# TensorE in the order of the text in the mixing stage of a two-layer decoder trunk, with more buffers for cached keys and values

## The chip, the cores and the metric

One core of one Trainium2 chip runs the whole kernel. The metric is the time of one execution on the device in microseconds (us); lower is better. The engines are TensorE (PE, matmuls; PEld is its loading of weights), VectorE (DVE), ScalarE (ACT), GpSimd (POOL) and SyncE (SP), whose queue issues most DMAs.

## What is computed

Two layers of a decoder, for 512 prompt tokens and 64 sample tokens (8 sequences of 8 new tokens, each with 2048 cached positions), model width 1024, hidden width 2816, all in fp32. Cut to what matters:

```python
def layer(x, l, k_past, v_past, s0):
    h = x + 0.5 * rmsnorm(swiglu(rmsnorm(x, ...), w_gate, w_up, w_down), ...)
    m, k_new, v_new, s_new = token_mixing(rmsnorm(h, ...), w_in[l], ..., w_out[l], k_past, v_past, s0)
    h = h + rmsnorm(m, ...)
    h = h + 0.5 * rmsnorm(swiglu(rmsnorm(h, ...), ...), ...)
    return h, k_new, v_new, s_new

def token_mixing(hn, w_in_l, ...):
    z = hn @ w_in_l                                  # 1024 -> 3584
    aq, ak, av, bq, bf, bi, bg = split(z)            # attention q k v, HGRN2 q f i g
    outs = [dilated_window(aq, ak, av, w, d) for (w, d) in ((128, 1), (512, 4), (2048, 16))]
    o_a = rmsnorm(dilated_mixture(outs), attn_g_l)   # 8 heads of 64
    f = lb_l + (1.0 - lb_l) * sigmoid(bf)
    o_b, s_fin = hgrn2_scan(silu(bq), 1.0 - f, bi, log(f), s_init, chunk)   # 4 heads of 128
    o_b = rmsnorm(o_b, hgrn_g_l) * silu(bg)
    return concatenate([o_a, o_b]) @ w_out_l, k_new, v_new, s_fin
```

For the sample tokens the attention's keys and values are the cached ones and the new ones, and HGRN2 starts from a given state.

## The kernel before

Activations lie with the features on the partitions and the tokens in the columns, in two halves of 288 tokens (256 of the prompt and 32 of the samples). Every weight and every operand of a product is split into two float32r parts, the high part on ACT (L114) and the low part on DVE (L116). A product then takes three matmuls per 128 rows of the contraction: high by high (L353), high by low (L354) and low by high (L355); with 1024 rows that makes 24 matmuls of 128x288. Weights come as items of 128 columns, in the order of use; SP loads an item (L95) and two loads stand ahead. `WBUF` items of split weights can be held, and `XBUF` more in a pool that exists outside the mixing stage only.

A layer is SwiGLU, mixing, the output projection and SwiGLU. The mixing stage runs 28 items of w_in (`run_phase` with lag 0): each item first for one half of the tokens, then for the other, so there are 56 calls of `issue`. One `issue` writes a product, the parked transposes (`flush_late`), the next weights' loads and splits (`w_ahead`), the product's evacuation (`evac`), and then `side`. Items 0 to 11 are attention's q, k and v, 12 to 23 the f, q and i of the four HGRN2 heads, 24 to 27 their gates.

`side` is where the other work of the stage comes in, from Python generators that are pulled a few steps at a time: four steps of the sample attention (`sample`), two of each of up to two HGRN2 heads (`hgrn`), two of the prompt attention (`prompt_unit`), one of the norm of attention's output. What is left when the items run out is pulled by `rest`.

- `sample` works on two sample sequences at a time: scores `sc` (L849) against cached keys, each cached tile `kv` 128x512 (256 KB) loaded by L815 (keys) and L818 (values) into one of `KVB` buffers; scores `scn` against the new keys, also L849; a maximum (L874) and an exponential over all 1344 columns (L875); transposes `ptps` (L884); `pov`, the product with the values (L904); its scaled copy `ob` (L910) and the transpose `otr` (L913).
- `hgrn` goes through one head in levels `lev` (blocks of 1 to 8 at L590, with L594 for the samples, 32 at L623, 64 at L631). After each level DVE rescales zq (L659) and POOL rescales zk (L661), and the next level reads both. Then `ktp` (L676), its copy `kt` (L677), `kv` (L687), and the head's end with the `pos` matmuls of 8 columns (L697).
- `prompt_unit` has scores `psc` (L765), softmax, transposes `ptp` (L780), the copy `pt` (L782 on DVE, L784 on ACT) and `ppv` (L789).

The order in which each engine issues is set by the tile framework's scheduler, which places every instruction by its own estimate; the text's order only serves it as a start. In the mixing stage it puts scores, levels and transposes between the matmuls of a product.

Of the kernel before, what the change touches and what calls it, by code (L numbers as in the profile page):

```python
# [9 lines left out]

F32 = mybir.dt.float32
F32R = mybir.dt.float32r
U8 = mybir.dt.uint8
AF = mybir.ActivationFunctionType
ALU = mybir.AluOpType
# [12 lines left out]
EPS = 1e-6  # L28
LAG = 3
GRP = 4  # L30
WBUF = 4
XBUF = 4
ZBUF = 2
ABUF = 2
KVB = 5
G_OFF = {}
_o = 0
for _n, _w in (("ff1_pre_g", 8), ("ff1_post_g", 8), ("mix_pre_g", 8), ("attn_norm_g", 4), ("hgrn_norm_g", 1),
# [9 lines left out]
def trunk_step(ctx: ExitStack, tc: tile.TileContext, a, L):  # L48
# [13 lines left out]
    ps_mm = ctx.enter_context(tc.tile_pool(name="ps_mm", bufs=2, space=PSUM))  # L62
    ps_hg = ctx.enter_context(tc.tile_pool(name="ps_hg", bufs=2, space=PSUM))

# [1 line left out]
    items = []  # L66
    for l in range(L):
        ff = {}
# [56 lines left out]
        while st["dma"] < min(st["split"] + 2, len(items)):  # L125
            w_dma()

# [1 line left out]
    def const(name, shape):  # L129
        return cp.tile(shape, F32, name=name)  # L130

# [34 lines left out]
    def late_consts():  # L166
        lstage = tmp("lstage")[:, :NLM * 32].rearrange("p (a b) -> p a b", b=32)
        for n, t in (("logits", logit), ("lmask", lstage), ("pbias", pbias), ("sb_str", sb_str), ("sb_rec", sb_rec),
                     ("sb_new", sb_new), ("bmask", bmask), ("eye32", eye32)):
            sp.dma_start(t if n == "lmask" else t[:], a[n])  # L170
        dve.tensor_copy(lmask[:], lstage)
        # lower bounds of the forget gates
        dve.tensor_copy(lbm[:], logit[:, 0, :])
        for l in range(1, L):
            dve.tensor_tensor(lbm[:], lbm[:], logit[:, l, :], op=ALU.max)
        for l in range(L):
            dve.tensor_tensor(lbe[:, l, :], logit[:, l, :], lbm[:], op=ALU.subtract)
        act.activation(lbe[:], lbe[:], AF.Exp)
        dve.tensor_copy(lbs[:], lbe[:, 0, :])
        for l in range(1, L):  # L180
            dve.tensor_tensor(lbs[:], lbs[:], lbe[:, l, :], op=ALU.add)
        dve.reciprocal(lbs[:], lbs[:])
        for l in range(L):
            dve.tensor_tensor(lbe[:, l, :], lbe[:, l, :], lbs[:], op=ALU.mult)
        dve.tensor_copy(lbm[:], lbe[:, 0, :])
        for l in range(L):
            if l:
                dve.tensor_tensor(lbm[:], lbm[:], lbe[:, l, :], op=ALU.add)
            dve.tensor_tensor(fof[:, l, :], lbm[:], lbe[:, 0, :], op=ALU.subtract)
            dve.tensor_scalar(fsc[:, l, :], fof[:, l, :], -0.5, 0.5, op0=ALU.mult, op1=ALU.add)  # L190
            dve.tensor_scalar(nfs[:, l, :], fsc[:, l, :], -1.0, None, op0=ALU.mult)
            dve.tensor_tensor(fof[:, l, :], fof[:, l, :], fsc[:, l, :], op=ALU.add)
# [2 lines left out]
    def tmp(name="tmp"):  # L195
        return tp.tile([P, H], F32, name=name, tag="tmp", bufs=6)

# [1 line left out]
    def stats(acc, inv, out_psum=False, tag="rb"):  # L199
        """rsqrt of the mean square of every token, on all partitions: [128, 288]"""  # L200
        s = ps_hg.tile([P, 512], F32, name="stat", tag="hg")
        for c in range(3):
            pe.matmul(s[:96, c:c + 1], acc[:, 96 * c:96 * c + 96], ones[:, 0:1], start=True, stop=True)
        sm = tp.tile([96, 4], F32, name="sm", tag="sm", bufs=2)
        dve.tensor_scalar(sm[:, :3], s[:96, :3], inv, EPS, op0=ALU.mult, op1=ALU.add)
        pool.tensor_tensor(sm[:, :3], sm[:, :3], nhalf[:96, :3], op=ALU.pow)  # L206
        yield
        b = ps_hg.tile([P, 512], F32, name="bc", tag="hg")
        for c in range(3):
            pe.transpose(b[:, 96 * c:96 * c + 96], sm[:, c:c + 1].to_broadcast([96, P]), ident[:96, :96])  # L210
        if out_psum:
            return b[:, :H]
        rb = tp.tile([P, H], F32, name="rb", tag=tag, bufs=1)
        act.activation(rb[:], b[:, :H], AF.Copy)
        return rb[:]

    class Chain:
        """what one half of the tokens goes through between two phases, issued in steps: jn tiles of the
        next operand are there, then its scale r"""

        def __init__(self, hf, gen):
            self.hf, self.jn, self.r, self.done = hf, 0, None, False
# [116 lines left out]
            c()  # L339

    def product(group, order=None, chain=None):
        """group: (psum, item, high, low); one tile of the contraction after the other, for all of them"""
        for _, i, _, _ in group:
            w_get(i)
        k = items[group[0][1]][1]
        order = order or range(k)
        for n, j in enumerate(order):
            s = slice(j * P, (j + 1) * P)
            if chain is not None:
                chain.until(n + 1)  # L350
            for ps, i, xhi, xlo in group:
                wh, wl = whi[i], wlo[i]
                pe.matmul(ps, wh[:, s], xhi[:, j, :], start=(n == 0), stop=False)  # L353
                pe.matmul(ps, wh[:, s], xlo[:, j, :], start=False, stop=False)  # L354
                pe.matmul(ps, wl[:, s], xhi[:, j, :], start=False, stop=(n == k - 1))  # L355
            if len(group) > 1 or n == k // 2 - 1:
                hook()

    def run_phase(n, operand, evac, chains, order=None, lag=LAG, side=None, on_done=None):
        """n items from items[st.next]; operand(i, hf) gives (psum, high, low), evac(i, hf, psum) takes the product"""  # L360
        i0 = st["next"]
        st["next"] += n

        def issue(idx, hf):
            group, tiles = [], []
            if idx[0] == 0:
                chains[hf].until(1)
            for i in idx:
                pst, xhi, xlo = operand(i, hf)
                group.append((pst[:, :H], i0 + i, xhi, xlo))  # L370
                tiles.append(pst)
            first = idx[0] == 0
            product(group, order if first else None, chains[hf] if first else None)
            flush_late()
            if hf == 0:
                w_ahead(i0 + idx[-1])
            else:
                w_ahead(i0 + idx[0])
            hook()
            if first:  # L380
                chains[hf].until_r()
            for i, pst in zip(idx, tiles):
                evac(i, hf, pst)
                if i == n - 1 and on_done is not None:
                    active.append(on_done(hf))
                if side is not None:
                    side(i, hf)

        g = list(range(GRP))
        issue(g, 0)  # L390
        issue(g, 1)
        for i in range(GRP, n):
            issue([i], 0)
            if i - lag >= GRP:
                issue([i - lag], 1)
        for i in range(max(GRP, n - lag), n):
            issue([i], 1)
        flush_late()

# [1 line left out]
    def swiglu(l, w, chains, gp, mk_chain, side=None):  # L401
        with ExitStack() as es:
            hpool = es.enter_context(tc.tile_pool(name="hid", bufs=1))
# [60 lines left out]
            run_phase(n, operand, evac, chains, side=side, on_done=on_done)  # L464
        return nxt

# [1 line left out]
    def mixing(l, chains, xpool_close, x_spill):  # L468
        o = [None, None]
        with ExitStack() as es:  # L470
# [39 lines left out]
            def evac(i, hf, pst):  # L510
                ps = pst[:, :H]
                r = rn[hf]
                if i < 8:
                    dst = (aq if i < 4 else ak)[:, i % 4, hf, :]
                    dve.tensor_tensor(dst, ps, r, op=ALU.mult)
                    if i == 7 and hf == 1:
                        late.append(lambda: sp.dma_start(a["o_k"][l], ak[:]))
                    return
                t = tmp("z")
                if i < 12 or (i < 24 and i % 3 == 2):  # L520
                    dve.tensor_tensor(t[:], ps, r, op=ALU.mult)
# [27 lines left out]
                    gates.append((h, hf, t))  # L549

            gates = []
            left = [12, 12]
            gated = [0, 0]
            normed = [False, False]
# [9 lines left out]
            hg_done = set()  # L564
            stage = [0] * 4

# [1 line left out]
            def pcol(t, c):  # L568
                return t[:, c // 2, (c % 2) * P:(c % 2) * P + P]

# [163 lines left out]
                hg_done.add(h)  # L734
                stage[h] = 4

# [1 line left out]
            def prompt_unit(p, i, alt):  # L738
                n = (i + 1) * P
                if alt == 1:  # L740
# [58 lines left out]
                    yield from prompt_unit(p, i, alt)  # L799
                    left[i // 2] -= 1  # L800

# [1 line left out]
            kvq = []  # L803
            kvs = {"n": 0}

# [132 lines left out]
            def side(i, hf):  # L938
# [10 lines left out]
                if i < 8:  # L949
                    return  # L950
                if i == 11 and hf == 1:
                    flush_late()
                    flags["av"] = True
                    prm.append(prompt(0))
# [17 lines left out]
                        if not pull(g):  # L972
                            hg.remove(g)

# [1 line left out]
            oa_g = g_of(l, "attn_norm_g")  # L976

            def anorm(hf):
# [43 lines left out]
            oc = [o_chain(0), o_chain(1)]  # L1022
            run_phase(28, operand, evac, chains, lag=0, side=side, on_done=lambda hf: oc[hf])
            tail["on"] = True
            while hg or prm or smp or alt or alt2 or an or gates:
                rest()
        return oc

    def w_out(l, chains, gp, mk_chain):
# [24 lines left out]
            run_phase(NJ, operand, evac, chains, on_done=on_done)  # L1054
        return nxt

# [1 line left out]
    xs = ExitStack()  # L1058

    def x_tiles():  # L1060
# [44 lines left out]
    xs.close()  # L1105


# [1 line left out]
def _tiles(w):  # L1109
    """(..., K, M) -> (..., M/128, 128, K): one contiguous [128, K/128 * 128] block for every 128 columns"""  # L1110
    *b, K, M = w.shape
    n = len(b)
    t = w.reshape(*b, K // P, P, M // P, P)
# [2 lines left out]


def _cols(v):
    """(L, n*128) -> (128, L, n)"""
    L = v.shape[0]  # L1120
    return np.transpose(v.reshape(L, -1, P), (2, 0, 1))

# [93 lines left out]
```

## Time and profile before

| | us |
|---|---|
| three runs | 2625.37, 2623.82, 2618.42 |
| median of the runs | 2623.82 |
| span of the profiled execution | 2620.2 |
| PE busy in it | 2570.6 (98%) |
| DVE, ACT, POOL busy | 1186.3, 900.4, 384.0 |
| the two mixing stages, as read below | 326.5 and 351.9 |

The profiled execution has no time of its own beside its span; the span stands 3.6 us under the median of the runs. "Busy" is the time in which an engine has an instruction under way; matmuls overlap, so a PE that is busy all the time can still start its matmuls at a greater or a smaller spacing. The row of an instruction gives its start, its duration, the engine and line, what it writes and reads, and in brackets how long its engine stood idle before it and what ended that.

### The profile page before, as it was taken

What the parts mean: (1) busy time and instruction counts of PE and PEld (TensorE: products, weight loads), DVE (VectorE), ACT (ScalarE), POOL (GpSimd) and SP (SyncE); (2) the same over time, 40 slices, a digit from 0 to 9 for tenths busy, and PEclk for the clock granted to TensorE, in tenths of its full rate; (3) what the DMA queues carried; (4) which work ended last, traced back from release to release, by engine and by line L of the source; (5) the groups of instructions that cost most, each with busy time, mean ns of one, the idle gap of its engine ahead of it and who ended that gap; (6) DMA issues with size and microseconds to landing.
All of it is one profiled execution on the core that took longest, in us unless ns stands there. A gap on an engine that the chain in (4) does not pass through costs nothing.

```text
span 2620.2 us, 52041 instructions
## 1 busy us (share of the span) xinstructions
PE 2570.6 (98%) x21844; PEld 2401.9 (92%) x21844; DVE 1186.3 (45%) x2648; ACT 900.4 (34%) x2023; POOL 384.0 (15%) x450
## 2 busy tenths in 40 slices
PE   8999999999999999999999999999999999999997
PEld 8999999867878999999999999997677799999997
DVE  6333346235555642434563334362456556324333
ACT  5232235133335532223532322342333254323232
POOL 1101012002212210101210010110022122101012
PEclk9999999999999999999999999999999899999998
DMA  5222223475543222222222222236754442222221
GB/s 177 81 81 81 89 74 109 159 240 172 167 155 130 82 89 81 83 87 76 78 89 81 81 81 89 74 108 190 223 186 156 131 145 73 87 83 74 89 81 44
DMA packets 108604, 292.03 MB, mean 111 GB/s; under 512 B 12753, under 2 KB 16081, under 8 KB 107601
## 3 DMA queue, kind: packets, MB, share of 16 engines
q1 hardware_dynamic: 107936, 288.28, 34.0%
q8 instruction: 172, 2.82, 0.4%
q14 instruction: 64, 0.52, 0.1%
q10 hardware_dynamic: 432, 0.41, 0.1%
HBM read 272.13 MB, written 16.52 MB: 110 GB/s over the span
## 4 chain that ended last, share of the span: by engine, by line
PE 90%; DVE 4%; issue 3%; DMA 1%; POOL 1%; ACT 1%; SPq 0%; POOLq 0%; ACTq 0%; DVEq 0%
PE gu L353 13%; PE gu L354 13%; PE gu L355 13%; PE mm L353 12%; PE mm L355 12%; PE mm L354 12%; PE sc L849 2%; PE pov L904 1%; PE psc L765 1%; PE ppv L789 1%; DMA kv<-in_kc 1%; DVE y L313 1%; POOL sm L206 1%; PE ptp L780 1%; DVE x L316 1%
## 5 line engine op out<-in xcount | busy, mean ns | idle before, releaser
L353 PE MATMUL gu<-xh,whi 128*128 128x288 f32 x2752 | 813.3, 296 | 7.1 <-ACT xh L269 6.3
L354 PE MATMUL gu<-xl,whi 128*128 128x288 f32 x2752 | 813.1, 295 | 0.0
L355 PE MATMUL gu<-xh,wlo 128*128 128x288 f32 x2752 | 811.2, 295 | 0.0
L114 ACT ACTIVATE whi<-wraw 128x512 fp32r<-128x512 f32 (+1 forms) x688 | 394.9, 614 | 758.3 <-PE gu L354 360.6
L116 DVE TENSOR_TENSOR wlo<-wraw,whi 128x512 fp32r<-128x512 f32 (+1 forms) x688 | 445.3, 680 | 194.7 <-ACT whi L114 176.9
L353 PEld LDWEIGHTS gu<-xh,whi 128*128 128x128 f32 x2752 | 517.9, 188 | 8.3 <-ACT xh L269 6.7
L355 PEld LDWEIGHTS gu<-xh,wlo 128*128 128x128 f32 x2752 | 518.9, 189 | 0.0
L354 PEld LDWEIGHTS gu<-xl,whi 128*128 128x128 f32 x2752 | 517.7, 188 | 0.5 <-DVE xl L270 0.5
L353 PE MATMUL mm<-hh,whi 128*128 128x288 f32 x1408 | 415.7, 295 | 0.0
L355 PE MATMUL mm<-hh,wlo 128*128 128x288 f32 x1408 | 414.7, 295 | 0.0
L354 PE MATMUL mm<-hl,whi 128*128 128x288 f32 x1408 | 414.7, 295 | 0.0
L434 POOL TENSOR_TENSOR gate<-gate,rb 128x288 f32<-128x288 f32 x176 | 163.8, 931 | 1287.8 <-ACT gate L433 1287.8
L353 PE MATMUL mm<-xh,whi 128*128 128x288 f32 x1088 | 334.9, 308 | 1.5 <-DVE y L449 1.5
L354 PE MATMUL mm<-xl,whi 128*128 128x288 f32 x1088 | 327.3, 301 | 0.0
L355 PE MATMUL mm<-xh,wlo 128*128 128x288 f32 x1088 | 327.3, 301 | 0.0
L355 PEld LDWEIGHTS mm<-hh,wlo 128*128 128x128 f32 x1408 | 264.7, 188 | 0.0
L354 PEld LDWEIGHTS mm<-hl,whi 128*128 128x128 f32 x1408 | 264.4, 188 | 0.0
L353 PEld LDWEIGHTS mm<-hh,whi 128*128 128x128 f32 x1408 | 264.2, 188 | 0.0
L438 DVE TENSOR_TENSOR hid<-gu,gate 128x288 f32<-128x288 f32 x172 | 78.7, 457 | 332.2 <-PE gu L355 323.6
L353 PEld LDWEIGHTS mm<-xh,whi 128*128 128x128 f32 x1088 | 205.3, 189 | 25.1 <-issue 21.4
L354 PEld LDWEIGHTS mm<-xl,whi 128*128 128x128 f32 x1088 | 205.4, 189 | 12.9 <-issue 12.4
L355 PEld LDWEIGHTS mm<-xh,wlo 128*128 128x128 f32 x1088 | 205.6, 189 | 12.6 <-issue 12.1
(193 smaller groups left out, 2430.0 us busy)
## 6 DMA issues: line engine op xcount, KB each, us to landing
wraw<-in_wgu SPq DMA_DIRECT2D x175, 512.0 KB, 3.4
kv<-in_kc SPq DMA_DIRECT2D x160, 256.0 KB, 3.4
kv<-in_vc SPq DMA_DIRECT2D x160, 256.0 KB, 3.3
wraw<-in_wd SPq DMA_DIRECT2D x64, 448.0 KB, 3.3
wraw<-in_w_in SPq DMA_DIRECT2D x56, 512.0 KB, 4.2
wraw<-in_wd SPq DMA_DIRECT2D x32, 512.0 KB, 3.5
wraw<-in_w_out SPq DMA_DIRECT2D x16, 512.0 KB, 4.4
xs<-x SPq DMA_DIRECT2D x4, 1152.0 KB, 4.2
```

The source lines that it names most:

```text
L114: act.activation(whi[i][:, c], r[:, c], AF.Copy)
L116: dve.tensor_tensor(wlo[i][:, c], r[:, c], f(whi[i][:, c]), op=ALU.subtract)
L206: pool.tensor_tensor(sm[:, :3], sm[:, :3], nhalf[:96, :3], op=ALU.pow)
L313: ins = dve.tensor_tensor(y[:, js, :], y[:, js, :], rb[:, None, :].to_broadcast([P, 2, H]), op=ALU.mult)
L316: dve.tensor_tensor(x[:, js, :], x[:, js, :], y[:, js, :], op=ALU.add)
L353: pe.matmul(ps, wh[:, s], xhi[:, j, :], start=(n == 0), stop=False)
L354: pe.matmul(ps, wh[:, s], xlo[:, j, :], start=False, stop=False)
L355: pe.matmul(ps, wl[:, s], xhi[:, j, :], start=False, stop=(n == k - 1))
L434: pool.tensor_tensor(g[:], g[:], rn[hf], op=ALU.mult)
L438: dve.tensor_tensor(h[:], ps, gate[hf][:], op=ALU.mult)
L765: pe.matmul(dst, q, kk, start=True, stop=True, tile_position=(64 * s, 0))
L849: pe.matmul(ps[32 * p:32 * p + 32, c], qbd[:, 2 * bp + bb, p, :], rhs(p), start=(bb == 0), stop=(bb == 1), tile_position=(0, 32 * p))
```

## The change

PE leaves the scheduler in most of the mixing stage: from `side` of item 11, second half, until everything of the stage has been pulled, `tc.manual_schedule` makes it issue in the order of the text. All other engines stay with the scheduler. `KVB` goes from five to nine buffers, so that eight loads stand ahead at the start of `sample`. `WBUF` goes from four to three and `XBUF` from four to five. From item 24 on, `evac` pulls `rest` as long as three gates or more are waiting. The constant `END` is 1, so its branch does nothing. Line numbers rise by one up to `evac` and by four behind its new loop (L353 is L354, L849 is L853, L904 is L908).

```diff
+END = 1
...
-WBUF = 4
-XBUF = 4
+WBUF = 3
+XBUF = 5
...
-KVB = 5
+KVB = 9
...
                     return
+                while i >= 24 and len(gates) >= 3:
+                    rest()
                 t = tmp("z")
...
             gates = []
+            man = ExitStack()
...
                 if i == 11 and hf == 1:
+                    man.enter_context(tc.manual_schedule(engines={mybir.EngineType.PE}))
                     flush_late()
...
             tail["on"] = True
+            if END == 0:
+                man.close()
             while hg or prm or smp or alt or alt2 or an or gates:
                 rest()
+            man.close()
         return oc
```

What this does to PE's order, at two places of layer 0. The first is in a run of score blocks of `sample`. A row is the line, the operation, what it writes and reads, the size and how many follow each other; `mm` are the product's matmuls, `sc` the scores, two matmuls for each cached tile. Before:

```order
L849 MATMUL sc<-kv,qbd 32x256 x2
L353 MATMUL mm<-xh_4516,whi 128x288
L354 MATMUL mm<-xl_4517,whi 128x288
L849 MATMUL sc<-kv,qbd 32x256 x2
L355 MATMUL mm<-xh_4516,wlo 128x288
L353 MATMUL mm<-xh_4516,whi 128x288
L354 MATMUL mm<-xl_4517,whi 128x288
L355 MATMUL mm<-xh_4516,wlo 128x288
L353 MATMUL mm<-xh_4516,whi 128x288
L354 MATMUL mm<-xl_4517,whi 128x288
L355 MATMUL mm<-xh_4516,wlo 128x288
L849 MATMUL sc<-kv,qbd 32x256 x2
```

And with the change:

```order
L354 MATMUL mm<-xh_4516,whi 128x288
L355 MATMUL mm<-xl_4517,whi 128x288
L356 MATMUL mm<-xh_4516,wlo 128x288
L853 MATMUL sc<-kv,qbd 32x256 x16
L784 MATMUL ptp<-ident,S 128x128 x2
L793 MATMUL ppv<-pt,vt 64x128 x2
L354 MATMUL mm<-xh_4716,whi 128x288
L355 MATMUL mm<-xl_4717,whi 128x288
```

The scores of eight cached tiles now stand in one row behind a whole product, and the prompt unit's `ptp` and the `ppv` that reads its copy stand next to each other, ahead of the next product.

The second place is at the last levels of HGRN2's first head. `lev` 32x32 is the level of 32, `lev` 64x64 the level of 64 of the same head. Before:

```order
L355 MATMUL mm<-xh_4716,wlo 128x288
L904 MATMUL pov<-kv,pts 32x128 x16
L623 MATMUL lev<-zq,zk 32x32 x8
L765 MATMUL psc<-ak,aq 128x256 x2
L353 MATMUL mm<-xh_4516,whi 128x288
L354 MATMUL mm<-xl_4517,whi 128x288
L355 MATMUL mm<-xh_4516,wlo 128x288
L353 MATMUL mm<-xh_4516,whi 128x288
L354 MATMUL mm<-xl_4517,whi 128x288
L631 MATMUL lev<-zq,zk 64x64 x4
L355 MATMUL mm<-xh_4516,wlo 128x288
```

And with the change:

```order
L356 MATMUL mm<-xh_4716,wlo 128x288
L908 MATMUL pov<-kv,pts 32x128 x16
L627 MATMUL lev<-zq,zk 32x32 x8
L635 MATMUL lev<-zq,zk 64x64 x4
L769 MATMUL psc<-ak,aq 128x256 x2
L354 MATMUL mm<-xh_4516,whi 128x288
L355 MATMUL mm<-xl_4517,whi 128x288
L356 MATMUL mm<-xh_4516,wlo 128x288
```

The second level, which stood behind two scores and five matmuls of the next product, now stands directly behind the first, and the product behind both.

## Rows read from the trace of the kernel before

**Rows 1.** The page: span, and busy time of the engines.

```profile
span 2620.2 us, 52041 instructions
...
PE 2570.6 (98%) x21844; PEld 2401.9 (92%) x21844; DVE 1186.3 (45%) x2648; ACT 900.4 (34%) x2023; POOL 384.0 (15%) x450
```

**Rows 2.** Mixing stages: stretch, us, busy PE, PEld, DVE, ACT, POOL, clock, DMA, GB/s.

```profile
497.00:823.50 326.50, 319.70 (x3664) 240.19 (x3664) 160.97 (x507) 108.52 (x305) 58.66 (x85) 0.99 0.55 177
1797.00:2148.90 351.90, 344.50 (x3834) 263.16 (x3833) 173.26 (x526) 122.38 (x331) 59.12 (x83) 0.98 0.55 175
```

**Rows 3.** Timeline of PE, scores inside a product: start, duration, engine, line, operation.

```profile
501.53 0.29 PE L353 MATMUL mm<-xh,whi 128*128 128x288 f32 x1
501.75 0.63 PE L849 MATMUL sc<-kv,qbd 128*32 128x256 f32 x4
502.31 0.40 PE L354 MATMUL mm<-xl,whi 128*128 128x288 f32 x1
502.54 0.30 PE L355 MATMUL mm<-xh,wlo 128*128 128x288 f32 x1
502.68 0.29 PE L353 MATMUL mm<-xh,whi 128*128 128x288 f32 x1
```

**Rows 4.** Timeline of PE, sixteen score passes in one piece.

```profile
650.76 1.07 PE L849 MATMUL sc<-kv,qbd 128*32 128x256 f32 x16
651.76 0.38 PE L210 MATMUL bc<-ident,sm 96*128 96x96 f32 x2
```

**Rows 5.** Timeline of PE, ppv inside a product.

```profile
609.20 0.65 PE L789 MATMUL ppv<-pt,vt 128*64 128x128 f32 x6
609.78 0.40 PE L355 MATMUL mm<-xh,wlo 128*128 128x288 f32 x1
610.02 0.29 PE L353 MATMUL mm<-xh,whi 128*128 128x288 f32 x1
```

**Rows 6.** Timeline of PE and DVE, from one level to the next of one head.

```profile
613.80 0.43 PE L623 MATMUL lev<-zq,zk 128*32 128x32 f32 x16
...
615.33 0.58 DVE L626 COPY A<-lev 32x128 f32<-32x128 f32 x2
...
615.92 0.49 DVE L659 TENSOR_TENSOR zq<-zq,d 128x128 f32<-128x128 f32 x2
...
616.36 0.42 PE L631 MATMUL lev<-zq,zk 128*64 128x64 f32 x4 [0.64 <-DVE zq L659]
```

**Rows 7.** Timeline of PE and DVE, a prompt unit's transpose and its copy.

```profile
607.86 0.33 PE L780 MATMUL ptp<-ident,S 128*128 128x128 f32 x1
...
608.23 0.42 DVE L782 COPY pt<-ptp 128x256 f32<-128x256 f32 x1
```

**Rows 8.** Timeline of PE and ACT, from scn over the exponential to ptps.

```profile
584.57 0.39 PE L849 MATMUL scn<-ak,qbd 128*32 128x64 f32 x10
...
585.82 1.42 ACT L875 ACTIVATE ss<-ss,smx 128x1344 f32<-128x1344 f32 x1 [0.51 <-DVE smx L874]
...
588.45 0.38 PE L884 MATMUL ptps<-ident,ss 128*128 128x128 f32 x2
```

**Rows 9.** Timeline of PE, a score that waited for its cached tile.

```profile
642.37 0.62 PE L849 MATMUL sc<-kv,qbd 128*32 128x256 f32 x4 [0.70 <-DMA kv<-in_kc]
```

**Rows 10.** The page, DMA issues: count, KB each, median us to landing.

```profile
kv<-in_kc SPq DMA_DIRECT2D x160, 256.0 KB, 3.4
```

**Rows 11.** PE in a short stretch: us, busy (count), granted clock, DMA share, GB/s.

```profile
2044.00:2057.00 13.00, 13.00 (x44) 0.50 0.41 133
```

**Rows 12.** Timeline of PE, ahead of that stretch and in it.

```profile
2040.82 1.95 PE L697 MATMUL pos<-zq,s 128*128 128x8 f32 x16
...
2053.22 0.44 PE L355 MATMUL mm<-xh,wlo 128*128 128x288 f32 x1
2053.46 0.44 PE L353 MATMUL mm<-xh,whi 128*128 128x288 f32 x1
```

## The prediction

> **What bounds the kernel now.** I read the head of the page first: the profiled execution spans 2620.2 us and TensorE (PE) is busy for 98% of it [rows 1]. Then the table of stretches, for the two mixing stages, the only places that the change touches: they last 326.5 and 351.9 us, and PE is idle for only 6.8 and 7.4 us of them [rows 2]. So the scheduler's order hides nearly every wait of the attention and HGRN2 chains behind product matmuls. Its price must be looked for inside the busy time, and the timeline shows it. Two product matmuls follow each other at .14 us (502.54 to 502.68). Where four score passes are put between them, 501.53 to 502.54 holds two products' spacing and the visit: 1.01 - .28 = .73 us [rows 3]. Sixteen score passes in one piece cost 1.00 us from their start to the next matmul, and .22 - .14 = .08 to get in, 1.08 us or .27 per four [rows 4]. (The trace shows a score matmul as two passes, so four passes are two matmuls, which read one cached tile.) A split visit thus costs .46 us more than its share of a gathered one, .23 per edge. After the other kinds an edge is cheaper: a product that follows ppv holds the next one off by .24 in place of .14, .10 more [rows 5].
>
> **What the change takes away.** Counted in the two lists of orders, per layer: the products stand in 110 pieces before and 56 after; runs of scores fall from 54 to 29; changes from one kind of matmul to another from 425 to 288, 137 fewer. Of these edges, 50 to 52 are of scores at .23 us, 12 us; the other 85 to 89 at .10, 9 us. Gain 21 us; all at .08 it is 11, all at .23 it is 32. Of PE's own 7 us of waiting I count 5 as gone (0 to 7), since the score block's loads now have eight tiles of lead. **Gain per layer 26 us, bounds 11 and 39.**
>
> **What it adds: waits that nothing covers.** In text order PE stops at each matmul whose operand is not there, and what stands behind it, the next product first of all, waits too, although it is ready. VectorE (DVE) and ScalarE (ACT) are 45% and 34% busy, so they don't bind; it is the latency of one chain that counts. I counted the pairs in which a matmul now stands right behind the one that feeds it, and took the price from the same chain in the trace of before.
> - *Level behind level of the same HGRN2 head*, 16 per layer: side pulls each head twice, so two levels stand next to each other, and the second reads the zq and zk that the first one's successors rescale. At 613.80 the level's passes run until 614.23, the copy and the rescaling on DVE take .58 and .49, and the next level starts at 616.36 [rows 6]. Bounds: the two DVE instructions alone, 1.07 us, and the whole gap, 2.13. I take 1.3, near the low end, because in that row other work stood ahead on DVE and will less often when PE itself waits: 21 us (17 to 34).
> - *ptp, then ppv* of a prompt unit, 16 per layer against 3: the copy of the transposed tile takes .42 on DVE; from the end of ptp at 608.19 to ppv at 609.20 it is 1.01 [rows 5, 7]. I take .7: 11 us (7 to 16).
> - *scn, then ptps* of a pair of sample batches, 3 per layer against none: a reduction and an exponential over 1344 columns lie between. The exponential alone takes 1.42 us, the whole gap is 588.45 - 584.96 = 3.49 [rows 8]. I take 2.5: 8 us (4 to 10).
> - *pov, ob, otr*, 8 per layer against none, and *ktp, kt, kv*, 4 per layer: a copy each, which I price by the .42 of the one between ptp and ppv [rows 7]; the wider kt has the two short ktps matmuls beside it. 12 x .42: 5 us.
> - *Cached keys*: sixteen score matmuls in one row read eight tiles of 256 KB, and 6 blocks per layer are such. Eight loads are under way in place of four, but a block frees all of its tiles at once and the next block stands one product piece later. Before, a late tile cost .70 [rows 9], and a load takes 3.4 us to land [rows 10]; below, nothing. I take .7 for each: 4 us (0 to 20).
>
> **Loss per layer 49 us, bounds 33 and 85.** Costed at nothing: three standing weight buffers for four, since with no lag between the halves only the item in use and the next are held, and outside mixing three and five make the same eight; if a split did wait for a buffer, its 512 KB and its ACT and DVE work would be late for a product, which the profile would name. On SP's queue the first cache loads are issued fourteen in a row and one w_in load (of item 14) moves behind the first 37 cache loads, but its product comes some three pieces of about 6 us each later (326.5 us over 56 pieces, [rows 2]), and a cached tile lands in 3.4; that cover gone, a product waits up to one landing. The new loop that drains gates from item 24 only moves the same pulls ahead of the last products. DVE, ACT and POOL keep the scheduler's order, with their work placed for the new PE order.
>
> **Sum.** 49 - 26 = 23 us more per layer, 46 for both: 2620.2 + 46 = 2666 for the profiled execution. The median of the runs shown, 2623.8, stands 3.6 above that span, so **2670 us**. The bounds of all terms together: 33 - 39 = -6 and 85 - 11 = 74 per layer, from 2612 to 2772; all ends falling on one side is unlikely.
>
> **The rivals.**
> - *Slower by the clock, too.* In the trace PE's granted clock falls to half, 1.2 of 2.4 GHz, for 13 us [rows 11], just after the 8-column matmuls of a head's end at 2040.82, and products then start .24 us apart, 2053.22 to 2053.46 [rows 12], in place of .14. With a stop in most blocks such stretches may become common: 33 pieces of 24 products, some 800, lie in the text-order part of a layer, and if half ran at the low clock, 400 x .10 = 40 us per layer, 80 in all on top of the forecast: about 2750. For it: the forecast puts a pause in nearly every block. Against: the 6.8 us of idle time of before brought no dip of their own; all dips there follow the narrow matmuls. The Trainium skill (TensorE: Matmul & The Clock Gate, section "A second HAM failure mode: psum-queue depth-cycling") describes this: PE that idles for moments between groups of matmuls swings between the two clock levels, and throughput suffers though a single matmul looks normal. The trace of before has no such groups, so it neither confirms nor excludes it.
> - *Slower by the loads.* If each of the 6 blocks waits out a landing of 3.4 us, the term is 20 in place of 4, 32 us more in all: about 2702. Against it: the stage's DMA share is .55 [rows 2].
> - *Faster: the waits are shared.* A pause lets DVE, ACT and POOL catch up, and the row between (another head's level, psc, stat) covers part. The point where it decides: waits under 26 us per layer, about half of my sum. At 20 us with a gain of 39, its high end, it is 19 us per layer, 38 in all: 2586 against the median; with my gain of 26 it is 6 per layer: 2612. In the middle, about 2600. For it: PE is idle almost nowhere, so every edge saved counts in full, and the low ends of my terms already make 33. Against: the pairs stand adjacent in the list, and their DVE work can't start sooner.
> - *No change*: waits within 4 us of the gain, or an order that moves less than the list seems to show. The list does differ, in half of its pieces.
>
> **How the numbers follow.** The forecast has .39, the clock .11, the loads .10; these three are slower by over 0.3%, .60 together. Faster by over .3% has .31, within it .09; 0.3% is about what a measurement of this kernel can tell from no change. Bounds of the range: up, the forecast with its terms near the high ends and the loads, 2735, without the clock's case; down, the faster rival nearly to its end, 2590. The forecast's own range is 2635 to 2715.
>
> **What would show it.** If right: PE idle in the mixing stretches rises from 7 us to between 30 and 60 per layer; the waits by line name lev after DVE zq or POOL zk most, then ppv after pt, ptps after ss; scores stand in rows of 32 passes; the stretches outside mixing stay within 2 us. If the clock decides, the granted clock of the mixing stretches falls from .99 to .9 or less. If the loads decide, the waits name kv<-in_kc with over 20 us. I am wrong if idle time in the mixing stretches stays under 26 us per layer, or if it rises so far while busy time falls by more.

## The result, and the profile after

The change makes the kernel slower: the median is 2702.4 us (four runs, 2698.7 to 2707.5) against 2624.6 us before in the same comparison. The ratio is 1.031, 95% interval 1.029 to 1.033. The forecast was 2670, within 2590 to 2735.

The head of the page after. Beside it [rows 1]: PE is busy for the same time as before, 2571.4 against 2570.6 us, but the span has grown by 79.7 us, 78.9 of it idle time by this view.

```profile
span 2699.9 us, 52036 instructions
...
PE 2571.4 (95%) x21844; PEld 2428.8 (90%) x21844; DVE 1191.2 (44%) x2648; ACT 899.5 (33%) x2023; POOL 381.5 (14%) x450
```

That the busy time stays is misleading, and the table of stretches shows why. Here are the two mixing stages from the first product of w_in to the first of the output projection, PE alone (length, busy time with count, granted clock, DMA share, GB/s). Before:

```profile
434.30:823.50 389.20, 380.37 (x4124) 0.99 0.52 168
1731.70:2124.00 392.30, 382.86 (x4124) 0.98 0.52 167
```

And after:

```profile
432.90:860.20 427.30, 379.98 (x4100) 0.92 0.46 151
1773.00:2200.60 427.60, 377.82 (x4101) 0.93 0.46 152
```

The stages are 38.1 and 35.3 us longer. The output projection right behind each takes 3.7 longer, since 24 matmuls that stood in the stage before (4124 against 4100) now run in it. (The second stretch of [rows 2] ran some 25 us into that projection, so it was not the stage alone; the idle time read from it is the same.) Idle time goes from 8.8 and 9.4 us to 47.3 and 49.8. The granted clock falls from .99 and .98 to .92 and .93. So PE saved time on its matmuls and lost about as much to the clock.

The granted clock has two levels, 1.2 and 2.4 GHz. Were a stretch at the lower one to do half of its work, span times (1 - mean granted clock) would be the time that the low clock takes. That is the most it can be, since some idle time lies in such stretches too, and since products there start .24 us apart in place of .14, not .28 [rows 12]. The view of the cores, before and after:

```profile
core 0: 2620.2 us, clock 0.994
```

```profile
core 0: 2699.9 us, clock 0.974
```

That gives .006 x 2620.2 = 15.7 us before and .026 x 2699.9 = 70.2 after. The change in three terms:

| us, whole span | before | after | difference |
|---|---|---|---|
| PE idle (span less busy) | 49.6 | 128.5 | +78.9 |
| low clock, at most | 15.7 | 70.2 | +54.5 |
| rest of the busy time, at least | 2554.9 | 2501.2 | -53.7 |
| span | 2620.2 | 2699.9 | +79.7 |

How far "at most" may be off can be estimated. These are the sums over all stretches at the low clock (length, and PE busy in them), before and after:

```profile
sum 33.95, PE 22.30; mean PE 5.57
```

```profile
sum 138.93, PE 119.97; mean PE 4.80
```

With .10 us lost of every .24, as between two products, 22.3 and 120.0 us of busy time lose 9 and 50. By this estimate the low clock took 41 us more, and the rest of the busy time fell by 40. The clock also differs from one execution of a kernel to the next: the four of the change have .972 to .977 (62 to 76 us by the table's reckoning), the kernel before .992 to .998. Differences of some 15 us in this term between two kernels are therefore not told by one profile.

What PE waited for, from the view of waits after (line that waited, releaser; us in total, times, longest):

```profile
PE ptps L888 <- ACT ss L879: 15.6, 6, 2.9
PE otr L917 <- ACT ob L914: 14.6, 16, 1.7
...
PE ppv L793 <- ACT pt L788: 6.5, 22, 0.3
...
PE lev L594 <- DVE s L730: 5.5, 6, 1.1
PE lev L635 <- DVE zq L663: 5.0, 6, 2.1
PE lev L635 <- POOL zk L665: 4.7, 8, 0.7
PE lev L594 <- POOL zk L645: 4.4, 2, 2.2
PE stat L204 <- DVE y L736: 4.0, 6, 0.8
PE tr L505 <- DVE mx L772: 3.9, 8, 0.8
PE ppv L793 <- DVE pt L786: 3.6, 13, 0.6
```

Each kind can be seen in the timeline. First scn, the exponential and ptps, and the next product (PE and ACT):

```profile
578.37 0.39 PE L853 MATMUL scn<-ak,qbd 128*32 128x64 f32 x10
...
580.08 1.42 ACT L879 ACTIVATE ss<-ss,smx 128x1344 f32<-128x1344 f32 x1 [0.63 <-DVE smx L878]
...
581.64 2.71 PE L888 MATMUL ptps<-ident,ss 128*128 128x128 f32 x11 [2.89 <-ACT ss L879]
...
584.28 0.80 PE L769 MATMUL psc<-ak,aq 64*128 64x128 f32 x4
...
585.46 0.69 PE L505 MATMUL tr<-ident,z 128*128 128x128 f32 x2 [0.39 <-DVE mx L772]
...
587.05 0.44 PE L355 MATMUL mm<-xl,whi 128*128 128x288 f32 x1
...
587.29 0.44 PE L356 MATMUL mm<-xh,wlo 128*128 128x288 f32 x1
...
591.83 0.30 PE L355 MATMUL mm<-xl,whi 128*128 128x288 f32 x1
...
591.97 0.29 PE L356 MATMUL mm<-xh,wlo 128*128 128x288 f32 x1
```

PE stands for 2.89 us; in [rows 8] the whole gap was 3.49. Then the product, which needs nothing of these, starts its matmuls .24 us apart; at its end they are .14 apart again. That is the low clock of [rows 12], here behind idle time, and a row of the stretch has it:

```profile
582.00:591.00 9.00, 8.62 (x37) 0.50 0.09 35
```

Then a pair of levels and a prompt unit:

```profile
593.09 0.46 PE L594 MATMUL lev<-zq,zk 128*32 128x32 f32 x31
...
595.30 0.46 PE L594 MATMUL lev<-zq,zk 128*32 128x32 f32 x32 [1.68 <-DVE zq L605]
...
595.76 0.44 PE L784 MATMUL ptp<-ident,S 128*128 128x128 f32 x2
596.51 0.43 PE L793 MATMUL ppv<-pt,vt 128*64 128x128 f32 x2 [0.32 <-ACT pt L788]
597.46 0.43 PE L793 MATMUL ppv<-pt,vt 128*64 128x128 f32 x2 [0.52 <-DVE pt L786]
597.82 0.40 PE L354 MATMUL mm<-xh,whi 128*128 128x288 f32 x1
```

Level behind level waits 1.68 us [rows 6], ppv twice, .32 and .52 [rows 5, 7]. The product at 597.82 reads none of these results and stands behind all three waits.

What PE did ahead of each low stretch can be read as well. In the mixing stages of the kernel before there are three, 20.5 us in all, each behind the narrow `pos` matmuls with no idle time. With the change there are 23, 122.9 us in all. Two of them are again such: sixteen passes of 8 columns, and then, behind a few other matmuls, the low clock:

```profile
2046.77 1.95 PE L701 MATMUL pos<-zq,s 128*128 128x8 f32 x16
```

```profile
2048.99:2052.40 3.41, 3.41 (x17) 0.50 0.84 283
```

Ahead of each of the other 21 PE had just stood waiting. So narrow matmuls bring the clock down in both kernels, and what the change adds lies behind waits. The kernel before has one such dip as well, at its end: the clock falls while PE waits 2.23 us, with no narrow matmul ahead.

```profile
2607.05 1.09 PE L203 MATMUL stat<-ones,acc 128*96 128x1 f32 x6 [2.23 <-DVE acc L260]
```

```profile
2606.73:2620.21 13.48, 1.83 (x9) 0.50 0.23 88
```

### The profile page after: what moved, and what is told of

Its sections match the earlier page's. It is cut to its first block, busy times and chain, and to the rows that moved or that the text cites. A ratio compares the mean times of both kernels' runs of the same rounds, so it can differ in the third digit from the quotient of the medians.

```text
span 2699.9 us, 52036 instructions
## 1 busy us (share of the span) xinstructions
PE 2571.4 (95%) x21844; PEld 2428.8 (90%) x21844; DVE 1191.2 (44%) x2648; ACT 899.5 (33%) x2023; POOL 381.5 (14%) x450
## 5 line engine op out<-in xcount | busy, mean ns | idle before, releaser
L354 PE MATMUL gu<-xh,whi 128*128 128x288 f32 x2752 | 812.8, 295 | 6.5 <-ACT xh L270 5.7
L354 PEld LDWEIGHTS gu<-xh,whi 128*128 128x128 f32 x2752 | 518.3, 188 | 7.6 <-ACT xh L270 6.0
L354 PE MATMUL mm<-hh,whi 128*128 128x288 f32 x1408 | 415.5, 295 | 0.0
L354 PE MATMUL mm<-xh,whi 128*128 128x288 f32 x1088 | 342.3, 315 | 1.5 <-DVE y L450 1.5
L354 PEld LDWEIGHTS mm<-hh,whi 128*128 128x128 f32 x1408 | 264.3, 188 | 0.0
L354 PEld LDWEIGHTS mm<-xh,whi 128*128 128x128 f32 x1088 | 213.5, 196 | 27.8 <-issue 24.4
L355 PEld LDWEIGHTS mm<-xl,whi 128*128 128x128 f32 x1088 | 213.9, 197 | 6.6 <-issue 6.6
L356 PEld LDWEIGHTS mm<-xh,wlo 128*128 128x128 f32 x1088 | 213.3, 196 | 0.8 <-issue 0.8
```

## The experiments

The theory that the trace suggests, A: text order makes waits that nothing covers, these bring the low clock down on the products behind them, and gathering gives back a part. Rivals: the other edits take part in the loss (B); the clock falls for another reason, or costs nothing (C); the chains are bound by DVE and POOL, so a wait that is covered only moves (D).

**e1, no text order.** The line that enters the manual schedule is left out; all other edits stay.

```diff
-                    man.enter_context(tc.manual_schedule(engines={mybir.EngineType.PE}))
```

> The changed kernel without its text order: nine cache buffers, three and five weight buffers and the gate loop, PE scheduled as before. Theory A (the text order alone makes the loss: waits that nothing covers, and the half clock that follows them): 2610 to 2630 us, as the kernel before; idle time of PE in each mixing stretch under 12 us, granted clock .98 or more. Rival B (buffers, weight buffers or the gate loop take part in the loss): above 2640 us.

Measured 2593.5 us, ratio .991 (.989 to .993), below the range of both. Idle time and clock of the stages are as A has them. B falls in its sign: the other edits don't lose, they gain some 26 us, which theory A had at nothing. The two mixing stages of e1 (columns as above):

```profile
432.70:808.00 375.30, 367.06 (x4124) 0.99 0.53 175
1717.00:2096.90 379.90, 371.89 (x4124) 0.98 0.52 173
```

Busy time falls by 13.3 and 11.0 us per stage, idle time and clock stay. The scores' group says where from (busy us, mean ns; idle before). Before, and e1:

```profile
L849 PE MATMUL sc<-kv,qbd 128*32 128x256 f32 x640 | 79.9, 393 | 5.8 <-DMA kv<-in_kc 5.1 <-issue 0.5
```

```profile
L853 PE MATMUL sc<-kv,qbd 128*32 128x256 f32 x640 | 58.9, 385 | 0.5 <-issue 0.4
```

The same 640 passes take 21 us less, and the 5.1 us of waiting for cached keys are gone. With more tiles at hand the scheduler gathers the scores by itself: 32 runs of them per layer in the list of orders, against 55 before (the prediction counts 54) and 29 in text order. So against the kernel that has the same buffers, the text order costs 2699.9 - 2592.1 = 108 us.

**e7, e1 with five cache buffers.**

```diff
-KVB = 9
+KVB = 5
```

> e1 with five cache buffers in place of nine: no text order, three and five weight buffers, the gate loop. If e1's 26 us come from the cache buffers (score runs per layer: 55 before, 32 in e1, 55 again here): 2612 to 2628 us, as the kernel before. If the weight buffers or the gate loop bring them: 2590 to 2605 us.

Measured 2617.5 us, ratio 1.000 (.999 to 1.001). The whole gain of e1 is the cache buffers', 24 us between these two medians. Weight buffers and gate loop cost and bring nothing that can be measured.

**e2, text order alone, on the kernel before.**

```diff
+            man = ExitStack()
...
                 if i == 11 and hf == 1:
+                    man.enter_context(tc.manual_schedule(engines={mybir.EngineType.PE}))
...
             while hg or prm or smp or alt or alt2 or an or gates:
                 rest()
+            man.close()
```

> The kernel before with the text order alone: five cache buffers, four and four weight buffers, no gate loop. Theory A: 2695 to 2720 us, no better than the change, with score blocks that wait for cached tiles (kv<-in_kc) for 5 to 20 us more than in the change, because eight tiles are read in one row and only five can be held. Rival B: under 2680 us, part of the change's loss came from the other edits.

Measured 2779.2 us, ratio 1.061 (1.059 to 1.064), far above the expectation. The loads' wait was undersized:

```profile
PE sc L850 <- DMA kv<-in_kc: 34.7, 26, 2.1
PE ptps L885 <- ACT ss L876: 15.6, 6, 2.9
PE otr L914 <- ACT ob L911: 14.1, 16, 1.7
```

The score blocks wait 34.7 us for cached keys, 1.9 in the change; the other waits are as there. Idle time is 161.0 us, 32.5 more than in the change, and the low clock takes .039 x 2780.9 = 108.5 at most, 38 more: the clock's price has grown with the idle time, and added about as much as the waits themselves. Text order needs the buffers more than the scheduler does: with five in place of nine it is some 80 us slower (spans of 2780.9 and 2699.9; e2 also keeps the weight buffers of before and has no gate loop), the scheduler 24 (e7 and e1).

**e3, PE kept busy while it waits.** Matmuls that nothing reads, into unused columns or ahead of the real result, stand in front of the waiting ones; no part of the computation is left out.

```diff
+    def fill(ps, n):
+        for _ in range(n):
+            pe.matmul(ps[:, 384:512], ident[:], ident[:], start=True, stop=True)
...
+                    fill(ps, 2 * flags["rep"])
...
+                fill(po, 1)
...
+                        if g == 0:
+                            fill(ps, 8)
...
+                        fill(ps, 2)
```

> The changed kernel with matmuls that nothing reads put ahead of the waiting ones (two of 128 columns ahead of a repeated level, one ahead of ppv, eight ahead of the first ptps of a pair of sequences, two ahead of otr), so that PE computes while it waits. The waits themselves stay. Theory A (the idle moments bring the half clock down on the products behind them, some 50 us of the 78): low-clock time in the mixing stretches falls from about 60 us each to under 25, and the time to 2655 to 2680 us although work was added. Rival C (the clock falls for another reason, such as the narrow matmuls, or it costs nothing): 2700 us or more.

Measured 2684.9 us, ratio 1.026 (1.024 to 1.028): 17 us less than the change by the medians, some 12 by the ratios to the kernel before (1.031 and 1.026), a little short of the expectation. It issues 384 passes more (192 matmuls), and is faster nevertheless. The first row is sixteen of them ahead of ptps in the timeline, the second the head of the page, the third the clock:

```profile
580.72 2.05 PE L69 MATMUL ptps<-ident 128*128 128x128 f32 x16
```

```profile
PE 2595.2 (97%) x22228; PEld 2454.8 (91%) x22228; DVE 1187.0 (44%) x2648; ACT 900.3 (34%) x2023; POOL 382.0 (14%) x450
```

```profile
core 0: 2683.2 us, clock 0.986
```

The two mixing stages of e3 (columns as above):

```profile
433.20:850.50 417.30, 389.25 (x4293) 0.97 0.46 155
1763.20:2184.30 421.10, 392.08 (x4292) 0.96 0.47 154
```

Their time at the low clock, summed over its stretches, falls from 65 and 58 us to 27 and 34, not quite to the 25 expected. Over the span the low clock takes .014 x 2683.2 = 37.6 us in place of 70.2, 32.6 less; all four executions have .986 or .987. Sixteen added passes last 2.05 us, so 384 are some 49; the rest of the busy time grows by 56.4, and idle time, in which most of that lies, falls by 40.5. Together 56.4 - 40.5 - 32.6 = -16.7. C falls for most of the loss: with work in a part of the same waits the clock stays up longer, so the idle moments brought it down, and the low clock costs real time. The narrow matmuls keep their share: 4 of the 14 low stretches in e3's mixing stages follow `pos` matmuls without idle time.

**e4, the side work in another order.**

```diff
+                pull_hg(1)
+                pull_all(prm, 1)
                 pull_all(smp, 4)
-                pull_hg(2)
-                pull_all(prm, 2)
+                pull_hg(1)
+                pull_all(prm, 1)
```

> The changed kernel with the side work pulled in another order: one step of the heads, one of the prompt unit, the four sample steps, then the second step of each, so that a level and ppv have the scores between them and what they wait for. Theory A: the waits of lev and ppv (43 us over both layers) fall to under 15, ptps and otr stay; with part of the clock's share the time is 2640 to 2670 us. Rival D (the chains are bound by DVE and POOL, and the wait only moves to the next row): 2690 us or more.

Measured 2605.9 us, ratio .996 (.995 to .998): 97 us below the change by the medians (90 by the ratios), twice what was expected, and a little below the kernel before. D falls. The lines of lev and ppv that are left among PE's waits (no row of ppv remains):

```profile
PE lev L594 <- DVE s L730: 5.0, 6, 0.8
...
PE lev L594 <- DVE zq L643: 1.0, 2, 0.5
...
PE lev L594 <- DVE zq L605: 0.9, 2, 0.5
```

Idle time falls by 54.7 us to 73.8: 36 of it are waits of lev and ppv, 11 those of stat and tr, which the expectation had left out, and the rest is mostly kv, otr and cached keys. The low clock falls by 25.9 to .017 x 2608.5 = 44.3, and the rest of the busy time by 11, which is within what one profile's clock can be off.

**e5, half of the side work in the middle of each product.**

```diff
+            if mid and n == k // 2 - 1:
+                mid[0]()
...
-                pull_all(smp, 4)
-                pull_hg(2)
-                pull_all(prm, 2)
+                    mid.append(drain)
+                pull_all(smp, 2 if mid else 4)
+                pull_hg(1 if mid else 2)
+                pull_all(prm, 1 if mid else 2)
```

> The changed kernel with half of the side work (two sample steps, one step of each head, one of the prompt unit) issued in the middle of each product and half behind it. By the list of orders the products then stand in 86 pieces per layer (55 in the change and in e4, 97 in e1). Theory A: every chain has half a product (1.6 us) over it, so idle time falls under 20 us per mixing stage (e4: 22), low clock with it, but some 30 more visits cost .2 to .46 us each, 6 to 14 us per layer: 2610 to 2635 us, above e4. Rival E (waits and clock are worth more than visits): under 2600 us.

Measured 2615.4 us, ratio .998 (.997 to 1.000). The time is as theory A has it, but neither of its two reasons came, so that is luck. Idle time did not fall below e4's: it is 22 and 24 us in the mixing stages against 22, and 80.2 over the span against 73.8. Two sample steps that follow each other still hold pov with otr and scn with ptps (13.0 and 15.7 us of wait, about as in e4), and tr waits 3.9 us as in the change. The rest of the busy time is 4 us above e4's, less than the 12 to 28 that 30 more visits per layer were to cost.

**e6, e4 with the sample steps interrupted at the two remaining waits.**

```diff
-                    yield
+                    yield "stop"
...
-                        yield
+                        yield "stop"
...
-                pull_all(smp, 4)
-                pull_hg(2)
-                pull_all(prm, 2)
+                pull_hg(1)
+                pull_all(prm, 1)
+                left_smp = pull_smp(4)
+                pull_hg(1)
+                pull_all(prm, 1)
+                pull_smp(left_smp)
```

The two yields are those behind the exponential and behind the copy `ob`; `pull_smp` ends at a "stop" and returns the steps that are left.

> e4 with the sample steps interrupted where ptps would wait for the exponential and otr for its copy: the second step of the heads and of the prompt unit comes in between, the left sample steps behind it. Theory A: ptps and otr waits (26 us over both layers) fall to about 8, low clock falls in part: 2575 to 2595 us, below e1. Rival D (the wait moves on to lev and ppv): 2600 us or more.

Measured 2583.9 us, ratio .987 (.985 to .990), as expected; it has the lowest median of all and beats both kernels. What is left of the two waits is 12 us, where about 8 were expected:

```profile
PE ptps L888 <- ACT ss L879: 9.5, 6, 2.3
...
PE otr L917 <- ACT ob L914: 2.4, 3, 0.9
```

All kernels in the three terms (us of the profiled span; low clock at most, rest at least, as above):

| kernel | PE idle | low clock | rest of busy | span |
|---|---|---|---|---|
| before | 49.6 | 15.7 | 2554.9 | 2620.2 |
| the change | 128.5 | 70.2 | 2501.2 | 2699.9 |
| e1 no text order | 46.2 | 20.7 | 2525.2 | 2592.1 |
| e7 e1, five cache buffers | 46.5 | 15.7 | 2552.9 | 2615.1 |
| e2 text order, five cache buffers | 161.0 | 108.5 | 2511.4 | 2780.9 |
| e3 waits filled with added matmuls | 88.0 | 37.6 | 2557.6 | 2683.2 |
| e4 respaced | 73.8 | 44.3 | 2490.4 | 2608.5 |
| e5 in halves | 80.2 | 39.2 | 2494.6 | 2614.0 |
| e6 respaced, with stops | 63.0 | 23.2 | 2496.1 | 2582.3 |

## Why the prediction was right, and where its sizes were off

- *The sign and the mechanism* were right: waits that the scheduler had covered stand open in text order, and they outweigh the gathering. e1 and e4 show it from two sides: without text order, and with the same text order but other work between the pairs, the loss is gone.
- *The waits.* Forecast 49 - 5 = 44 us per layer net, 88 in all; measured 78.9. By kind, over both layers and against the waits of before: lev 28 (forecast 42), ptps 16 (16), otr and kv 16 (10), ppv 10 (22), cached keys -3 (8, less the 10 of PE's own waits that were to go). Stat and tr, which the forecast did not name, make 10. Levels were priced too high: 28 us over 32 pairs is at most .9 each, where I took 1.3 and had 1.07 as the lowest; the eight waits of L635 on POOL, for one, were .7 us at most. The copy between pov and otr was priced too low: its 16 waits are .9 on the mean, where I took .42. Priced too high was ppv, whose 35 waits come in pairs for the two copies, .29 us on the mean (10.1 over 35).
- *The gathering.* Forecast 21 us per layer, 42 in all; the rest of the busy time fell by 53.7 at most, by 40 by the estimate from the products' spacing. The edge prices were about right. Which part the text order has is another matter: e1 gets 30 of the 54 from the cache buffers under the scheduler, and e2 gets 43 from the text order with five buffers. Both gather the same scores, which is the likely reason that the two gains don't add.
- *The cache buffers.* They entered the sum only as part of the 5 us of PE's own waits. Alone they are worth 24 to 26 us, by way of the scheduler's order, as e1 and e7 show. The list of orders of the change could not tell this, because text order hides it.
- *The step that failed is the clock.* It stood as a rival with a chance of .11 and a price of 80 us for half of the products; the forecast itself had it at nothing. It took 54.5 us at most, some 41 by the estimate, and without it the span would have grown by 25 to 39, so the sign holds without it. The forecast's 46 us were 34 short of the 79.7 measured: the clock's term was left out, and the other two together were 7 to 21 too high, which hid a part of that. That the range still holds the result is luck: its upper end, 2735, was drawn for the other terms and without the clock. The reason against the clock, that before all dips followed the narrow matmuls, was drawn from a trace in which PE idles for 9 us per stage, so it could not speak about 50; and it overlooked the dip at that trace's end, which begins in a wait. Here the Trainium skill (TensorE: Matmul & The Clock Gate, section "A second HAM failure mode: psum-queue depth-cycling") was the better guide: short idle moments between groups of matmuls make the clock swing and cost throughput. This case's traces agree: mean clock .974 with 128.5 us of idle time, .986 when part of that is filled with useless work (e3), .991 when it is covered with useful work (e6).
- *The loads as a bound* did not come: 1.9 us in the change. With five buffers the rival would have been true, 34.7 us (e2).
- *The signs named ahead.* Idle time in the mixing stages, 47 and 50 us, lies in the 30 to 60 forecast. Lev waited most, but ptps and otr came next, and ppv behind them. The granted clock of .92 and .93 stands between the .99 of the forecast and the .9 at which the clock was to decide.
- The 0.4% between e1 and e6 (2593.5 and 2583.9 us, each against the kernel before in its own comparison) is about as large as their intervals, .989 to .993 and .985 to .990, which meet at their ends. All four executions of e6 (2581.4 to 2589.3) are faster than all four of e1 (2589.6 to 2596.8), so e6 is likely the faster; what it gains over the scheduler with the same buffers is some 10 us.

## What to carry to other kernels

A hand-set order on an in-order engine has to be read pair by pair: wherever a matmul stands right behind the one that feeds it, the chain's latency is paid in the open (2.89 us between scn and ptps here), and everything ready behind it pays too. Here it was enough to put work that was there anyway between the two halves of each pair, 90 us or more for six changed lines. Count the clock with the waits: PE's busy time stayed the same to 1 us while a saving and a loss of 40 to 54 us each cancelled in it, so read the granted clock of the stretch beside the busy time. And try an edit's parts alone: the buffers would have been the gain, and the order hid it.

## What the runs showed of the hardware

The granted clock fell although no single wait of PE in the mixing stages of the change was over 2.9 us and most were under 1 us. From kernel to kernel the low-clock price broadly went with the idle time (46 us of idle time and 21 of price in e1, 63 and 23 in e6, 74 and 44 in e4, 128.5 and 70 in the change, 161 and 108 in e2), but not by it alone: e3, with 88 us of idle time, has 38. That 192 matmuls whose results nobody reads make the kernel 12 to 17 us faster (e3) was not expected from any view of the kernel before.
